# Hybrid HGRN2 and Mamba-2 layer: row sums of squares in quarters of a PSUM bank with their roots by way of DRAM, the first block's splits on VectorE, inputs loaded one step ahead

## Chip, core and metric

One core of a Trainium2 chip runs the whole layer in one launch. The metric is device time in microseconds (us) of one execution; a smaller time is better. TensorE (PE) multiplies, VectorE (DVE), ScalarE (ACT) and GpSimd (POOL) work elementwise, and SyncE (SP) only issues DMAs, one after the other.

## What is computed

One decoder layer over 2048 tokens of width 1024, all in float32. An RMS norm, one input projection, two mixers side by side (an HGRN2 gated linear recurrence with 8 heads, and a Mamba-2 scan with 16 heads in two groups), each with a norm and a gate of its own, one output projection, the residual, a last RMS norm. Cut to what matters:

```python
h = rmsnorm(x, norm_w[l])
proj = jnp.einsum('bsd,de->bse', h, w_in[l])
q_raw, f_raw, i_raw, g_raw, z, xbc, dt_raw = jnp.split(proj, split_idx, axis=-1)
hg_out = hgrn2_mix(...)    # o * rsqrt(mean(o*o over a head's 128) + EPS) ...
m2_out = mamba2_mix(...)   # y * rsqrt(mean(y*y over a group's 512) + EPS) ...
mix = jnp.concatenate([hg_out, m2_out], axis=-1)
x = x + jnp.einsum('bse,ed->bsd', mix, w_out[l])
return rmsnorm(x, final_norm_w)      # rmsnorm: x * rsqrt(mean(x*x over 1024) + EPS) * w
```

Three kinds of row sums of squares occur ahead of the output projection: over 1024 of the input (one for each token), over 128 of each HGRN2 head, and over 512 of each Mamba-2 group.

## The kernel before

**Tiles.** Tokens lie along the free axis, 512 to a block, four blocks. Each 128 columns of the input projection are one weight tile; `proj` (L376) multiplies it with the block's input as 24 matmuls of 128x512. Float32 is kept by splits: a value is cast to a high part (ACT) and the rest is a subtraction (DVE or POOL), and three products of parts are added: high with high, low weight with high input, high weight with low input. `hh` and `hl` are the parts of the input, `wh` and `wl` those of a weight. In the first block the weights come raw from DRAM (`wr`), are split in `w_emit` (L128 is the subtraction; GpSimd does it for the Mamba-2 tiles and for one more) and are saved to DRAM; later blocks load the parts.

**Units.** A block is a list of jobs (`block_jobs`): `H(hd)` is one HGRN2 head (projections `pf`, `pq`, `pg`), `M(ct)` two Mamba-2 heads (`px`, `pz`), `VV(q)` the values of four HGRN2 heads (`pv`, four steps over four banks), `B(g)` a Mamba-2 group's B and C (`pB`, `pC`), `dt_unit` its time steps (`dt`). Each unit gives projections at once and later stages with due numbers (`DUES`, `MDUES`), counted in projections: stage `m0` of a head runs 3 projections after the head began, and so on. A head's stages are two levels of products inside a chunk (bank `A` by `m0b`, bank `B` by `m2`), a transpose `kT` (`mk`), the state `hS` (`m5`) and the output `o` (`m6`). Tile's scheduler then sets each engine's final order.

**First block.** Its first head runs on input that is not yet normed (`hr`, `lr`), since the row factors aren't ready: `row_factors` sums the squares on ACT and DVE, `ss` is the sum over partitions on PE, two POOL steps make the root, and `spread_factors` makes the row vector `rawrs` by a matmul with a diagonal (`dg_hr`, bank `hb`). Then `prep(0, x0)` scales the input and splits it anew (`x`, `hh`, `hl`) before `dt` can start.

**Next block's input.** While a block runs, `stats(tb+1)` (L319) loads the next input (`xa`), squares it and adds it up, and `prep(tb+1)` (L339) loads it again (`xb`), scales it by the row factors `prs` and splits it. Both take their loads where they use them, from the pool of three `raw` buffers that the weights use too. `prs` comes from a diagonal and a matmul (bank `hb`).

**Row sums.** `ss_cols` (L144) makes four 128x2 matmuls with the squares as the stationary operand, for the input (`ss`) and for each Mamba-2 group (`mss`). The Mamba-2 roots lie in `nst`, are transposed (`rgt`) and go to DRAM (`rg_store`, L931). The HGRN2 heads do it another way (`m7`, L883): four heads' sums in four quarters of one bank (`hss`, 32 columns of 1/128 each as stationary operand), one row of each quarter to DRAM, back folded over 128 partitions, the root on POOL, and back to DRAM, from where the output projection reads it spread over partitions.

The four output blocks follow the mixers; their matmuls are `po`.

Of the kernel before, what the change touches and what calls it, by code (L numbers as in the profile page):

```python
# [38 lines left out]
def hybrid_layer(ctx, tc, xT, wt, wdt, wout, small, out):
# [36 lines left out]
    mean32 = cp.tile([P, 32], F32, name="mean32")  # L76
    G.memset(mean32, 1.0 / P)
# [37 lines left out]
    def w_emit(i):  # L115
# [12 lines left out]
        (G if i == 2 or c >= 32 else V).tensor_tensor(lo, raw, hi.bitcast(F32), op=ALU.subtract)  # L128
# [190 lines left out]
    def stats(tb):  # L319

        box = {}

        def part(c):
# [15 lines left out]
    def prep(tb, xs=None):  # L339
# [3 lines left out]
        def part(c):  # L343
            if c == 0:
                if xs is None:
# [4 lines left out]
                else:  # L350
# [9 lines left out]
            for k in range(2):  # L360
# [146 lines left out]
    def m2_unit(tb, g, c, ws, bcs, dts, sq, nst, r):  # L507
# [760 lines left out]
```

## Time and profile before

| | |
|---|---|
| time, median of 3 runs | 1876.06 us (1873.55 to 1876.25) |
| profiled execution, its own time | 1876.26 us |
| its span, first to last instruction | 1874.5 us |
| PE busy | 1840.6 us, 98% of the span |
| DVE busy | 1204.3 us, 64% |
| ACT busy | 735.7 us, 39% |
| POOL busy | 315.3 us, 17% |
| mean granted TensorE clock | 0.993 of full speed |

Busy times are of one engine each and overlap. An instruction on PE that had to wait shows how long PE stood idle before it and which instruction of which engine released it. The page's strip of the granted clock shows full speed in nearly every slice, 9 tenths or less in the first and 8 tenths in the second.

### The profile page before, as it was taken

What the parts mean: (1) busy time and instruction counts of PE and PEld (TensorE: products, weight loads), DVE (VectorE), ACT (ScalarE), POOL (GpSimd) and SP (SyncE); (2) the same over time, 40 slices, a digit from 0 to 9 for tenths busy, and PEclk for the clock granted to TensorE, in tenths of its full rate; (3) what the DMA queues carried; (4) which work ended last, traced back from release to release, by engine and by line L of the source; (5) the groups of instructions that cost most, each with busy time, mean ns of one, the idle gap of its engine ahead of it and who ended that gap; (6) DMA issues with size and microseconds to landing.
All of it is one profiled execution on the core that took longest, in us unless ns stands there. A gap on an engine that the chain in (4) does not pass through costs nothing.

```text
span 1874.5 us, 33134 instructions
## 1 busy us (share of the span) xinstructions
PE 1840.6 (98%) x12910; PEld 1519.9 (81%) x12910; DVE 1204.3 (64%) x2951; ACT 735.7 (39%) x1303; POOL 315.3 (17%) x388
## 2 busy tenths in 40 slices
PE   7899999899999999999999999999999999999997
PEld 5688888788888888888888888888888877888887
DVE  7678868956576478556764885476457764534445
ACT  4546545533353245234433543353333532211113
POOL 1432243311011212120112221201121130000000
PEclk9899999999999999999999999999999999999999
DMA  7676877754555556456555655555565375424241
GB/s 277 245 274 233 299 258 251 257 182 157 176 187 202 180 180 225 142 176 191 175 201 182 194 195 202 171 191 166 172 193 168 113 235 171 163 84 154 92 148 46
DMA packets 112605, 351.83 MB, mean 188 GB/s; under 512 B 14464, under 2 KB 17184, under 8 KB 111936
## 3 DMA queue, kind: packets, MB, share of 16 engines
q1 hardware_dynamic: 111344, 348.46, 55.3%
q8 instruction: 102, 1.67, 0.4%
q10 hardware_dynamic: 1104, 1.26, 0.2%
q14 instruction: 55, 0.45, 0.1%
HBM read 269.69 MB, written 79.97 MB: 187 GB/s over the span
## 4 chain that ended last, share of the span: by engine, by line
PE 91%; DVE 5%; DMA 2%; issue 1%; ACT 1%; POOL 0%; DVEq 0%; SPq 0%; ACTq 0%
PE po L1100 16%; PE pz L384 9%; PE px L384 9%; PE pg L384 9%; PE pf L384 9%; PE pq L384 8%; PE pv L629 8%; PE pB L384 2%; PE pC L384 2%; PE yd L578 2%; PE yo L589 1%; PE hS L856 1%; PE S L569 1%; PE o L875 1%; PE o L874 1%; PE A L691 1%
## 5 line engine op out<-in xcount | busy, mean ns | idle before, releaser
L1100 PE MATMUL po<-mh,woh 128*128 128x512 f32 x480 | 188.9, 395 | 0.1
L1100 PE MATMUL po<-mh,wol 128*128 128x512 f32 x480 | 186.8, 390 | 0.0
L1100 PE MATMUL po<-ml,woh 128*128 128x512 f32 x480 | 186.1, 390 | 0.8 <-DVE ml L1089 0.8
L1100 PEld LDWEIGHTS po<-mh,woh 128*128 128x128 f32 x480 | 90.1, 188 | 22.0 <-issue 1.7
L828 POOL COPY att<-atq 32x128 f32<-32x128 f32 x128 | 63.2, 493 | 261.1 <-DVE atq L713 257.2
L1100 PEld LDWEIGHTS po<-ml,woh 128*128 128x128 f32 x480 | 89.9, 188 | 20.5 <-DVE ml L1089 1.9
L1100 PEld LDWEIGHTS po<-mh,wol 128*128 128x128 f32 x480 | 90.1, 188 | 18.9 <-issue 0.7
L1088 ACT CAST mh<-mr 128x1024 fp32r<-128x1024 f32 x33 | 34.6, 1051 | 166.3 <-PE po L1100 146.5
L471 DVE SCALAR_TENSOR_TENSOR xs<-u_x,sm,xs 128x512 f32<-128x512 f32 x96 | 71.9, 749 | 14.5 <-ACT xs L469 14.2
L542 DVE TENSOR_SCALAR csb<-csb,cs 128x128 f32<-128x128 f32 x256 | 65.2, 327 | 23.9 <-ACT ecs L539 23.9
L1089 DVE TENSOR_TENSOR ml<-mr,mh 128x1024 fp32r<-128x1024 f32 x31 | 37.8, 1220 | 65.6 <-ACT mh L1088 65.6
L865 DVE SCALAR_TENSOR_TENSOR hSt<-hgS,totw,hS 128x128 f32<-128x128 f32 x32 | 11.1, 346 | 95.4 <-PE hS L856 95.4
L629 PE MATMUL pv<-wh,hh 128*128 128x512 f32 x224 | 71.2, 399 | 0.0
L629 PE MATMUL pv<-wl,hh 128*128 128x512 f32 x224 | 69.5, 391 | 0.0
L629 PE MATMUL pv<-wh,hl 128*128 128x512 f32 x224 | 69.0, 389 | 0.0
L384 PE MATMUL px<-hh,wh 128*128 128x512 f32 x256 | 68.4, 410 | 0.0
L384 PE MATMUL pz<-hh,wh 128*128 128x512 f32 x256 | 67.4, 405 | 0.0
L601 POOL TENSOR_TENSOR sqa<-sqa,ecs 128x512 f32<-128x512 f32 x24 | 34.2, 1424 | 190.4 <-ACT ecs L600 190.4
L384 PE MATMUL pg<-hh,wh 128*128 128x512 f32 x248 | 65.4, 405 | 0.0
L384 PE MATMUL pf<-hh,wh 128*128 128x512 f32 x248 | 64.7, 403 | 0.0
L384 PE MATMUL pq<-hh,wh 128*128 128x512 f32 x248 | 64.7, 401 | 0.0
L128 POOL TENSOR_TENSOR wl<-wr,wh 128x1024 fp32r<-128x1024 f32 x21 | 53.8, 2563 | 64.6 <-ACT wh L127 63.3
(356 smaller groups left out, 4635.1 us busy)
## 6 DMA issues: line engine op xcount, KB each, us to landing
wh<-whd SPq DMA_DIRECT2D x156, 512.0 KB, 4.4
wl<-wld SPq DMA_DIRECT2D x156, 512.0 KB, 3.5
whd<-wh SPq DMA_DIRECT2D x52, 512.0 KB, 4.7
wld<-wl SPq DMA_DIRECT2D x52, 512.0 KB, 3.9
wr<-wt SPq DMA_DIRECT2D x51, 512.0 KB, 5.1
mr<-mixd SPq DMA_DIRECT2D x66, 256.0 KB, 2.9
csb<-csd SPq DMA_DIRECT2D x32, 512.0 KB, 5.6
rgh<-rgd SPq DMA_DIRECT2D x34, 256.0 KB, 3.2
```

The source lines that it names most:

```text
L128: (G if i == 2 or c >= 32 else V).tensor_tensor(lo, raw, hi.bitcast(F32), op=ALU.subtract)
L384: state["mm"] = T.matmul(ps, lhsT=a[:, k, :], rhs=b[:, k, :], start=(n == 0), stop=(n == 23))
L471: V.scalar_tensor_tensor(dst, u[:, j:j + TB], cw[:, c, j:j + 1], dst, op0=ALU.mult, op1=ALU.add)
L542: V.tensor_scalar(csb[:, i, w, :], csb[:, i, w, :], dts["cs"][:, w, h0 + i:h0 + i + 1], 0.0, ALU.subtract, ALU.min)
L569: T.matmul(pS[:, sl], lhsT=bc["Bn"][:, w, :], rhs=xdc[:, sl], start=True, stop=True)
L578: T.matmul(pd[64 * i:64 * i + 64, w * P:(w + 1) * P], lhsT=xdt[:, w * P + i * 64:w * P + i * 64 + 64], rhs=csb[:, i, w, :], start=True, st ...
L601: G.tensor_tensor(sq["acc"], sq["acc"], t, op=ALU.add)
L629: T.matmul(ps, lhsT=a[:, 2 * j + k, w * P:(w + 1) * P], rhs=rhs, start=(j == 0 and n == 0), stop=(j == 3 and n == 5))
L828: G.tensor_copy(att[qs, :, qs], r["atq"][qs])
L1088: A.copy(mh[:, :, 0:n], mr[:, :, 0:n])
L1089: lo.tensor_tensor(ml[:, :, 0:n], mr[:, :, 0:n], mh[:, :, 0:n].bitcast(F32), op=ALU.subtract)
L1100: T.matmul(pss[d], lhsT=a[:, d, :], rhs=b, start=(first and n == 0), stop=(e == (HE - 1 if bl == LAST else 15) and n == 2))
```

## The change

All sums of squares but the first block's input go the way of the heads: one function, `row_roots`, takes up to four sums, puts each into a quarter of a bank by a matmul with 32 columns of 1/n, and takes the roots by way of DRAM. The next input's sum shares a bank with the first Mamba-2 group's; the second group's goes alone, in the last block with the first's. The row factors `prs` are read from DRAM, spread over partitions, and no longer made by a diagonal and a matmul. The input parts of `stats` and `prep` are loaded one step ahead of their use. In the first block all weight splits and the low parts of the normed input are on DVE, the first head's later stages have due numbers of their own, the row factors are made inside `pg`, `dt` has a bank of the larger pool, and the last step of `VV` ends its four banks in another order.

```diff
+RDUES = (3, 4, 7, 9, 10, 11, 12, 13)
...
-        (G if i == 2 or c >= 32 else V).tensor_tensor(lo, raw, hi.bitcast(F32), op=ALU.subtract)
+        V.tensor_tensor(lo, raw, hi.bitcast(F32), op=ALU.subtract)
...
+    def row_roots(nm, tb, row, accs, keep):
+        n = len(accs)
+        ps = bank(nm)
+        for j, (acc, m) in enumerate(accs):
+            T.matmul(ps[32 * j:32 * j + 32, :], lhsT=means[m], rhs=acc, start=True, stop=True)
+        A.copy(keep[0:32 * n, :], ps[0:32 * n, :])
+        flat = rg_d[tb][row * NW:(row + n) * NW, :].rearrange("w t -> (w t)")
+        nc.sync.dma_start(flat.rearrange("(j t) -> j t", j=n),
+                          keep[0:32 * n, :].rearrange("(j r) t -> j r t", r=32)[:, 0, :])
+        rc = mp.tile([P, 16], F32, tag="rc", bufs=2, name=f"rc{nm}")[:, 0:NW * n]
+        fold = flat.rearrange("(p c) -> p c", c=NW * n)
+        nc.sync.dma_start(rc, fold)
+        rstd_cols(rc, rc, 1)
+        nc.sync.dma_start(fold, rc)
...
     stats:
-                x_rstd(tb, ss_cols(acc, bank(f"ss{tb}")))
-        return [lambda c=c: part(c) for c in range(4)]
+                row_roots(f"ss{tb}", tb - 1, R0, [(sq[0]["acc"], 512), (acc, D)], acc)
+        def at(c):
+            load(c + 1)
+            if c >= 0:
+                part(c)
+        return [lambda c=c: at(c) for c in range(-1, 4)]
...
     prep:
-                    ps = bank(f"hb{tb}")
-                    bcast_cols(rsx[:, tb, :], None, ps, f"h{tb}")
-                    box["rs"] = slot("s", [TB], f"prs{tb}")
-                    A.copy(box["rs"], ps)
...
-                E = V if kk % 2 else G
+                E = V if kk % 2 or xs is not None else G
...
+        def at(c):
+            if xs is None and c < 0:
+                box["rs"] = slot("s", [TB], f"prs{tb}")
+                nc.sync.dma_start(box["rs"].rearrange("p (w t) -> p w t", w=NW),
+                                  rg_d[tb - 1][RX * NW:(RX + 1) * NW, :].partition_broadcast(P))
+            if xs is None and c < 3:
+                box[c + 1] = xr = wp.tile([P, 2, TB], F32, tag="raw", bufs=3, name=f"xb{tb}_{c + 1}")
+                nc.sync.dma_start(xr, xT[tb, :, 2 * c + 2:2 * c + 4, :])
+            if c >= 0:
+                part(c)
...
     proj:
+                if inside and n == 12:
+                    inside()
...
     dt_unit:
-            ps = pj.tile([P, TB], F32, tag="pj", name=f"dt{tb}")
+            ps = bank(f"dt{tb}")
...
     m2_unit:
         def m3():
-            ssv = ss_cols(sq["acc"], bank(f"mss{nm}"))
-            ss = mp.tile([P, NW], F32, tag="mss", bufs=2, name=f"mss{nm}")
-            V.tensor_copy(ss, ssv)
-            rstd_cols(nst[:, g, :], ss, 512)
+            accs = [(sq["acc"], 512)]
+            if tb == NTB - 1:
+                accs.append((sqs[0]["acc"], 512))
+            row_roots(f"mss{nm}", tb, R1, accs, sq["acc"])
...
     v_step:
-            for w in ((1, 2, 0, 3) if tb in raw_rs else range(NW)):
+            for w in ((0, 3, 1, 2) if j == 3 else (1, 2, 0, 3) if tb in raw_rs else range(NW)):
...
     hg_unit:
-            row_factors(tb, x0)
...
-            held["g"] = proj(hts[tb], w_get(ws[2]), f"pg{nm}", bank(f"pg{nm}"))
+            held["g"] = proj(hts[tb], w_get(ws[2]), f"pg{nm}", bank(f"pg{nm}"), lambda: row_factors(tb, x0))
...
-        return [pf_raw, pq_raw, pg_raw] if raw else [pf, pq, pg], list(zip(DUES, (m0, m0b, m1, m2, mk, m5, m6, m7)))
+        return [pf_raw, pq_raw, pg_raw] if raw else [pf, pq, pg], list(zip(RDUES if raw else DUES, (m0, m0b, m1, m2, mk, m5, m6, m7)))
...
-        add(rg_store, tb, nst)
```

**Where the first block's first head ends.** PE, from the last values' matmuls on: `B` is the head's second level, `kT` its transpose, `dt` the first use of the normed input, `pB` the next projection. Before:

```order
L629 MATMUL pv_0_3_557<-wh_629,lr_307 128x512 x2
L691 MATMUL B_0_772<-MB_0_0_661,k_0_528 32x48 x16
L819 MATMUL B_0_772<-hq_0_672 32x32 x8
L823 MATMUL B_0_772<-qa_0_673,k_0_485 64x64 x4
L403 MATMUL dt_818<-hh_533,wd 32x512 x8
L403 MATMUL dt_818<-hl_534,wd 32x512 x8
L390 MATMUL kT_0_837<-ident,k_0_485 128x128 x4
L384 MATMUL pB_0_892<-hh_533,wh_698 128x512 x4
```

And with the change:

```order
L666 MATMUL pv_0_2_556<-wh_629,lr_307 128x512 x2
L439 MATMUL dt_772<-hh_533,wd 32x512 x8
L439 MATMUL dt_772<-hl_534,wd 32x512 x8
L418 MATMUL pB_0_839<-hh_533,wh_667 128x512 x4
L451 MATMUL dtn_791<-sel,dT_789 128x16 x4
L418 MATMUL pB_0_839<-hh_533,wh_667 128x512 x4
L418 MATMUL pB_0_839<-hh_533,wl_668 128x512 x8
L418 MATMUL pB_0_839<-hl_534,wh_667 128x512 x8
L727 MATMUL B_0_874<-MB_0_0_741,k_0_528 32x48 x16
```

`dt` and `pB` now come before `B`, and `kT` (not shown) stands after `pC`.

The same place on DVE, where `x` is the scaling of the normed input, `hl` its low part, `wl` a weight's split, and `MB`, `tot`, `k` belong to the head's second level. Before:

```order
L365 TENSOR_TENSOR hl_534<-x_1_297,hh_533 128x512
L713 COPY_PREDICATED atq_0_617<-mask_506,A_0_584 128x16x4
L771 TENSOR_TENSOR MB_0_0_661<-MB_0_0_523,tot_0_0_526 128x16x4x2
L773 TENSOR_TENSOR MB_0_0_661<-MB_0_0_523,tot_0_0_526 128x16x4x4
L721 TENSOR_TENSOR tot_0_0_526<-tot_0_0_526 128x64
L362 SCALAR_TENSOR_TENSOR x_2_300<-x_2_300,sm,rawrs_482 128x512
L722 TENSOR_TENSOR tot_0_0_526<-tot_0_0_526 128x64
L362 SCALAR_TENSOR_TENSOR x_2_300<-x_2_300,sm,rawrs_482 128x512
```

And with the change:

```order
L388 TENSOR_TENSOR hl_534<-x_1_297,hh_533 128x512
L385 SCALAR_TENSOR_TENSOR x_2_300<-x_2_300,sm,rawrs_482 128x512 x2
L131 TENSOR_TENSOR wl_668<-wr_669,wh_667 128x1024
L388 TENSOR_TENSOR hl_534<-x_2_300,hh_533 128x512 x2
L385 SCALAR_TENSOR_TENSOR x_3_303<-x_3_303,sm,rawrs_482 128x512 x2
L131 TENSOR_TENSOR wl_706<-wr_707,wh_705 128x1024
L388 TENSOR_TENSOR hl_534<-x_3_303,hh_533 128x512 x2
L807 TENSOR_TENSOR MB_0_0_741<-MB_0_0_523,tot_0_0_526 128x16x4x2
```

The whole normed input is split before the second level begins; two weight splits and all low parts, which POOL had a share of, stand among it.

**Where the first block's last heads run.** SP's queue around the load of the last part of the next input, `xb_3`; `mixd` are stores of finished outputs, `whd` and `wld` saves of weight parts. Before:

```order
L94 DMA whd_131<-wh_3859 128x1024
L880 DMA mixd_0_226<-sg_0_3130 128x512
L95 DMA wld_183<-wl_3860 128x1024
L595 DMA mixd_0_258<-y_0_3663 128x512
L356 DMA xb_3_4004<-xT 128x1024
L328 DMA xa_0_6089<-xT 128x1024
```

And with the change:

```order
L399 DMA xb_3_3786<-xT 128x1024
L97 DMA whd_95<-wh_3692 128x1024
L129 DMA wr_3798<-wt 128x1024
L98 DMA wld_147<-wl_3693 128x1024
L129 DMA wr_3849<-wt 128x1024
L97 DMA whd_119<-wh_3796 128x1024
```

The load has moved ahead of three more weight loads and of the stores of `sg` and `y`.

DVE ahead of the last head's `k`, which `kT` on PE needs; `csb` is a Mamba-2 decay. Before:

```order
L743 TENSOR_TENSOR tot_7_0_3997<-f_0_3806 128x256
L362 SCALAR_TENSOR_TENSOR xb_3_4004<-xb_3_4004,sm,prs_3369 128x512 x2
L542 TENSOR_SCALAR csb_0_3587<-csb_0_3587,cs_997 128x128 x8
L365 TENSOR_TENSOR hl_3372<-xb_3_4004,hh_3371 128x512
L546 TENSOR_TENSOR csb_0_3587<-csb_0_3587,BC_0_2697 128x1024
L713 COPY_PREDICATED atq_0_3698<-mask_515,B_0_3894 128x4x24
L833 TENSOR_TENSOR k_0_3382<-k_0_3382,tot_6_0_3796 128x4x64
```

And with the change:

```order
L779 TENSOR_TENSOR tot_7_0_3985<-f_0_3794 128x256
L579 TENSOR_SCALAR csb_0_3575<-csb_0_3575,cs_974 128x128 x8
L131 TENSOR_TENSOR wl_3939<-wr_3940,wh_3938 128x1024
L583 TENSOR_TENSOR csb_0_3575<-csb_0_3575,BC_0_2685 128x1024
L749 COPY_PREDICATED atq_0_3686<-mask_515,B_0_3882 128x4x24
L869 TENSOR_TENSOR k_0_3370<-k_0_3370,tot_6_0_3784 128x4x64
```

The two `xb` steps and the `hl` stand further ahead in the queue now, and one weight split stands here instead.

## Rows read from the trace of the kernel before

**Rows 1.** The page's first part: busy time of each engine.

```profile
PE 1840.6 (98%) x12910; PEld 1519.9 (81%) x12910; DVE 1204.3 (64%) x2951; ACT 735.7 (39%) x1303; POOL 315.3 (17%) x388
```

**Rows 2.** PE's timeline, first 80 us: start, duration, instruction, count, [idle before].

```profile
21.55 1.98 PE L384 MATMUL pq<-lr,wh 128*128 128x512 f32 x8
25.17 1.02 PE L148 MATMUL ss<-ones,pacc 128*128 128x2 f32 x8 [1.65 <-DVE pacc L303]
26.05 3.67 PE L384 MATMUL pg<-hr,wh 128*128 128x512 f32 x8
...
33.20 1.02 PE L168 MATMUL hb<-dg_hr,ones 128*128 128x512 f32 x2
...
61.09 0.44 PE L819 MATMUL B<-hq 128*32 128x32 f32 x16 [2.75 <-DVE hq L797]
...
65.09 3.59 PE L403 MATMUL dt<-hh,wd 128*32 128x512 f32 x8 [2.38 <-ACT v L635]
...
71.59 1.17 PE L384 MATMUL pB<-hh,wh 128*128 128x512 f32 x4
```

**Rows 3.** DVE's timeline, first 70 us.

```profile
17.20 2.90 DVE L303 TENSOR_TENSOR pacc<-pacc,sq 128x512 f32<-128x512 f32 x1
...
27.82 0.88 DVE L167 TENSOR_SCALAR dg_hr<-ident,rsx 128x128 f32<-128x128 f32 x4 [1.06 <-POOL rsx L142]
...
48.82 2.79 DVE L365 TENSOR_TENSOR hl<-x,hh 128x512 fp32r<-128x512 f32 x1
...
51.66 0.28 DVE L771 TENSOR_TENSOR MB<-MB,tot 128x128 f32<-128x128 f32 x1
...
61.80 1.24 DVE L806 TENSOR_TENSOR tot<-tot 128x8 f32<-128x8 f32 x1
```

**Rows 4.** Line 128, weight splits: count, ns min/median/max, first and last start.

```profile
L128 DVE TENSOR_TENSOR wl<-wr,wh x30: 1204/1220/2237, 15.3 to 351.4; 128x1024 fp32r<-128x1024 f32 x30
L128 POOL TENSOR_TENSOR wl<-wr,wh x21: 2375/2401/3387, 16.3 to 363.8; 128x1024 fp32r<-128x1024 f32 x21
```

**Rows 5.** Windows: length, busy PE, PEld, DVE, ACT, POOL; clock, DMA.

```profile
34.88:65.08 30.20, 24.27 (x214) 19.15 (x213) 29.59 (x56) 14.00 (x26) 13.19 (x6) 0.92 0.58 209
190.00:220.00 30.00, 30.00 (x278) 25.38 (x277) 27.89 (x65) 14.70 (x23) 10.82 (x6) 1.00 0.79 283
```

**Rows 6.** PE's timeline near the first block's end.

```profile
372.58 1.12 PE L390 MATMUL kT<-ident,k 128*128 128x128 f32 x4 [4.74 <-DVE k L833]
373.70 3.75 PE L384 MATMUL px<-hh,wh 128*128 128x512 f32 x8
```

**Rows 7.** DVE's timeline at the same place.

```profile
363.46 3.55 DVE L362 SCALAR_TENSOR_TENSOR xb<-xb,sm,prs 128x512 f32<-128x512 f32 x2 [1.98 <-DMA xb<-xT]
```

**Rows 8.** SP's queue at the same place.

```profile
358.77 0.45 SPq L356 DMA_DIRECT2D xb<-xT  x1
```

**Rows 9.** PE's timeline around row sums and a spread in the first block.

```profile
243.74 1.07 PE L890 MATMUL hss<-on,mean 128*32 128x512 f32 x8
...
250.32 0.95 PE L148 MATMUL mss<-ones,sqa 128*128 128x2 f32 x8
251.13 0.63 PE L390 MATMUL tB<-ident,BT 128*128 128x128 f32 x4
...
317.93 1.02 PE L168 MATMUL hb<-dg_h,ones 128*128 128x512 f32 x2
318.39 2.16 PE L384 MATMUL pq<-hh,wh 128*128 128x512 f32 x7
```

**Rows 10.** DMA issues: queue, count, KB each, us to landing.

```profile
rc<-rgd SPq DMA_DIRECT2D x8, 8.0 KB, 3.1
rgh<-rgd SPq DMA_DIRECT2D x34, 256.0 KB, 3.2
```

**Rows 11.** POOL's timeline: the root of four heads' sums.

```profile
257.93 2.89 POOL L142 TENSOR_TENSOR rc<-rc,mhalf 128x16 f32<-128x16 f32 x1
```

**Rows 12.** PE's waits by what it waited for: total, times, longest.

```profile
PE yo L589 <- DVE hgS L865: 2.1, 1, 2.1
```

More of the change, by code (lines that the diff above doesn't have):

```diff
@@ L75, in hybrid_layer @@
     G.memset(mhalf, -0.5)
-    mean32 = cp.tile([P, 32], F32, name="mean32")
-    G.memset(mean32, 1.0 / P)
+    means = {}
+    for n in (P, 512, D):
+        means[n] = cp.tile([P, 32], F32, name=f"mean{n}")
+        G.memset(means[n], 1.0 / n)
     epst = cp.tile([P, 1], F32, name="epst")
@@ L317, in scaled, with stats, load @@
         return dst
-    def stats(tb):
+    def stats(tb, sq):
         box = {}
+        def load(c):
+            if c < 4:
+                box[c] = xr = wp.tile([P, 2, TB], F32, tag="raw", bufs=3, name=f"xa{tb}_{c}")
+                nc.sync.dma_start(xr, xT[tb, :, 2 * c:2 * c + 2, :])
         def part(c):
@@ L344, in part @@
             if c == 0:
[L345 to L350 removed]
+                if xs is not None:
                     box["rs"] = raw_rs[tb]
@@ L367, in part @@
                 new_hts[tb] = (hh, hl)
-        return [lambda c=c: part(c) for c in range(4)]
+        def at(c):
[8 more added lines that the diff above has]
+                part(c)
+        return [lambda c=c: at(c) for c in range(-1, 4)]
     new_hts = {}
@@ L374, in use, with proj @@
         hts[tb] = new_hts[tb]
-    def proj(h, w, name, ps=None):
+    def proj(h, w, name, ps=None, inside=None):
         hh, hl = h
@@ L887, in m7 @@
                 return
-            ps = bank(f"hss{nm}")
-            for j in range(4):
-                T.matmul(ps[32 * j:32 * j + 32, :], lhsT=mean32, rhs=sqs[j], start=True, stop=True)
-            rr = sqs[3]
-            A.copy(rr, ps)
-            flat = rg_d[tb][(hd - 3) * NW:(hd + 1) * NW, :].rearrange("w t -> (w t)")
-            nc.sync.dma_start(flat.rearrange("(j t) -> j t", j=4), rr.rearrange("(j r) t -> j r t", r=32)[:, 0, :])
-            rc = mp.tile([P, 16], F32, tag="rc", bufs=2, name=f"rc{nm}")
-            fold = flat.rearrange("(p c) -> p c", c=16)
-            nc.sync.dma_start(rc, fold)
-            rstd_cols(rc, rc, 1)
-            nc.sync.dma_start(fold, rc)
-        return [pf_raw, pq_raw, pg_raw] if raw else [pf, pq, pg], list(zip(DUES, (m0, m0b, m1, m2, mk, m5, m6, m7)))
+            row_roots(f"hss{nm}", tb, hd - 3, [(a, P) for a in sqs], sqs[3])
+        return [pf_raw, pq_raw, pg_raw] if raw else [pf, pq, pg], list(zip(RDUES if raw else DUES, (m0, m0b, m1, m2, mk, m5, m6, m7)))
     pend = []
@@ L990, in block_jobs @@
         M(4)
+        call(nxt[4])
+        nxt = prep(tb + 1) if tb + 1 < NTB else [lambda: None, lambda: None, early_mix, lambda: None, lambda: None]
         H(5)
-        nxt = prep(tb + 1) if tb + 1 < NTB else [lambda: None, early_mix, lambda: None, lambda: None]
+        call(nxt[0])
         M(5)
-        call(nxt[0])
+        call(nxt[1])
         H(6)
-        call(nxt[1])
+        call(nxt[2])
         M(6)
-        call(nxt[2])
+        call(nxt[3])
         H(7)
-        call(nxt[3])
+        call(nxt[4])
         M(7)
-        add(rg_store, tb, nst)
         return out_
@@ L1027, in hybrid_layer @@
     low_part(0, x0)
-    again = prep(0, x0)
+    again = prep(0, x0)[1:]
     def consts():
```

32 lines of the change are left out of this document (11 added, 21 removed).

## Prediction

> **What bounds the kernel now.** I read the page's busy times first: PE is busy 98% of the span, DVE 64%, POOL 17% [rows 1]. So a microsecond goes only where PE stands idle, runs at half its clock, or has less to do. PE's timeline says where it is idle: in the first 70 us, ahead of `ss` (1.65), ahead of the second level's `B` (2.75) and ahead of `dt` (2.38) [rows 2], and once near the first block's end, ahead of `kT` (4.74) [rows 6]. By the table of waits, what remains is short, the longest 2.1 ahead of the last block's `yo` [rows 12]. Third, the clock: eight 128x512 matmuls take 3.67 in `pg` right after the first wait, but 1.98 in `pq` before it [rows 2]; half the clock, as after `kT` (3.75) [rows 6]. Last come the engines that PE waits for: DVE is busy 29.59 of the 30.20 us in which the first block's input is normed, POOL works beside it [rows 5], and the weight splits are shared by the two [rows 4].
>
> The sum is made against the profiled execution, 1876.26 us, 1.76 more than its span; the median of the runs is 1876.06.
>
> **A. The first 72 us.** `pq` ends at 23.53 (21.55 + 1.98) [rows 2]. `ss` is now issued inside `pg`, so `pg` starts there, unbroken by the wait and so at the full clock, which I take as 3.67 / 2 = 1.84 for eight. `ss` stands behind 15 of its 24 matmuls, at 23.53 + 15 x 0.229 = 27.0. It finds its operand ready: `pacc` ended shortly before 25.17 [rows 2]; two splits newly ahead of it on DVE add 2.4 [rows 4]; but one `pacc` took 2.90 [rows 3] where a 128x1024 split, twice its size, takes 1.22 [rows 4], so some 2.2 of it was POOL's split in the way, and goes. 25.1 + 2.4 - 2.2 = 25.3, under 27.0; with the stretch kept, 27.5, half a microsecond of wait. The chain from `ss` by the POOL root to the diagonal's end takes what it took, 25.17 to 28.70 (27.82 + 0.88) [rows 2, 3], 3.5: `hb` at 30.5, not 33.20. PE's stretch from `hb` to the values' end lasted to 61.09 - 2.75 = 58.34, 25.1, of which some 0.5 is a group of `B` that now comes later (I take the 0.44 of the next one); hence 55.2 [rows 2]. `dt` no longer waits for its bank. Its 16 matmuls take 16 x 0.229 = 3.7 at the full clock, not 3.59 for eight [rows 2]: `pB` starts at 58.9, not 71.59, 12.7 earlier. Owed afterwards are 28 small products of `B` (at 0.44 for 16: 0.8) [rows 2] and `kT` (half its 1.12) [rows 6], 1.3. **A = 11.4.**
>
> That needs DVE in time. `f` began 1.7 after `hb`, at 34.88 [rows 2, 5], so now at 32.2. Of the 30.2 us that followed, the second level leaves: 20 instructions from `MB` at 51.66 to `tot` at 61.80 [rows 3], 8.9 by their durations, 4.3 of it stretched in the same way. POOL's stretch of one split (2237 against 1220) [rows 4] and one `hl` (2.79 against some 0.6 for half a split's elements) [rows 3] goes, 3.2. Four low parts and two splits come, 4 x 0.6 + 2 x 1.2 = 4.8. So 30.2 - 8.9 - 3.2 + 4.8 = 22.9, and the last `hl` is there at 55.1. `dt` wants it in its second half, at 57.0: 1.9 to spare. The second level follows after `dt` and `pB`, and its output has `pC` and the next unit as cover. Bounds: if no stretch goes but falls on other steps, the last `hl` comes 3.2 + 4.3 later, 62.6, and 5.6 of A is lost, leaving 5.8; if `B`'s products also cost nothing more, 12.7. I stay at 11.4, the value of the rows at hand.
>
> **B. The wait for `kT`.** `k` on DVE was late by 4.74 [rows 6]. In its queue ahead of it DVE waited 1.98 for a load of `xb` and then scaled it for 3.55 [rows 7]; SP had issued that load only at 358.77, behind stores of finished outputs [rows 8]. The change puts the load a step ahead, and the two `xb` steps and the `hl` leave this place; one split of 1.2 comes in [rows 4]: 1.98 + 3.55 - 1.2 = 4.3 of the 4.74 go, and 0.4 stays. With the wait the half clock behind it goes: 3.75 - 1.98 in `px`, half of `kT`'s 1.12 [rows 2, 6], 2.3. 4.3 + 2.3 = 6.6; I add 0.3, since part of 0.4 may fall to `hl`. **B = 6.9.** Bounds: 7.1 (all gone), and 3.5 when half of it turns up again as a wait for another DVE step, since DVE has the same work to do somewhere.
>
> **C. PE's own work on row sums.** Removed: 8 `mss` and 3 `ss`. One of them took 0.95, but kept the next instruction back by 0.81 (250.32 to 251.13); a spread `hb` by 0.46 (317.93 to 318.39), three go; the transposes `rgt` some 0.1 [rows 9]. 11 x 0.81 + 3 x 0.46 + 0.1 = 10.4. Added: four pairs and three singles. No row shows them; the nearest are four quarters at 1.07 (`hss`) and one full-width matmul of the same 512 columns at 0.46 [rows 9]. Eight passes in a row would be 8 x 0.23 = 1.84, so quarters overlap, at 1.07 for four. I take 0.46 for a single and 0.66 for a pair (a third of the way from one to four): 4.0. **C = 10.4 - 4.0 = 6.4.** Bounds: 7 x 0.46 = 3.2 and 7 x 1.07 = 7.5, so 7.2 to 2.9.
>
> The Trainium skill speaks against the low price ("TensorEngine Tiling (Array Packing)", Tiling Modes, Key Properties): tiles work independently and in parallel, and a switch of the tiling mode drains TensorE. By it one quarter costs what four do, and most of 1.07 is the drain. The overlap of four quarters agrees; what one costs no row shows. The gain would be 3.5 less.
>
> **What I cost at nothing.** Splits on DVE: 21 x 1.22 = 25.6 comes in over the first block [rows 4]. A window of it shows DVE busy 27.89 of 30 us, so 2.1 free, and POOL 10.82 [rows 5]; but the 21 POOL splits took 2.4 each, in which DVE's own steps were stretched (1.0 in the longest split, 2.2 in one `hl`) [rows 3, 4]. At 1.2 lost for each the exchange is even, and I take it so. Without that, rival 2. The roots by DRAM: a store, a load, a root, a store, a spread load, each landing in 3.1 to 3.2 [rows 10], with POOL's 2.89 [rows 11]: some 16 us. SP issues in order, so weight loads behind a waiting store wait too; in the first block they are issued well over ten us ahead of use, and the heads' chain already has such a store. The sums of the input are done some 20 us before `prep` reads `prs`. The last wait of the kernel, `yo` (2.1) [rows 12], isn't touched; for the range it may go.
>
> **Sum.** 11.4 + 6.9 + 6.4 = 24.7; 1876.26 - 24.7 = **1851.6**.
>
> **Rivals.**
> *One quarter costs like four (1855.1).* C is 2.9: 1876.26 - 11.4 - 6.9 - 2.9. For it: only the four together are on record. Against it: nothing but the full-width 0.46. By the Trainium skill's rule above this is the case that holds.
>
> *Waits move rather than leave (1860.5).* DVE's long steps are not POOL's doing, or ACT or a load is late next: A is 5.8, B 3.5, C 6.4. For it: DVE is full in this stretch [rows 5], and 1.9 is a thin margin. Against it: the long steps stand where POOL's splits run.
> The Trainium skill ("SBUF — State Buffer", SBUF: two separate sides) calls the port pair that DVE and GpSimd share a lock held for a whole instruction, the other blocked; the 2.90 of `pacc` agrees, and by that rule the stretch goes with POOL's splits and this rival falls.
>
> *DVE becomes the bound of the first block (1874.6, the same).* If the splits' 25.6 us on DVE are not paid back by shorter steps, its 2.1 in 30 cover 23 over some 330 us when evenly spread, and nothing where it is full already. Between 2.6 and 25.6 I take 14.1: 1860.5 + 14.1. The change then does not do what it says for the splits. Against it: the 2237 of one split.
>
> *The root's chain holds SP's queue (1880, slower).* Four DMAs for each of three `prs`, each held in SP's queue behind another transfer: 4 x (3.2 + 3.2 + 1) + 2.9 = 32.5 rather than 16 [rows 10, 11], 12.5 past the 20 at hand; with the wait's half clock some 9.5 of it is PE's, for three blocks 28.5. 1851.6 + 28.5 = 1880.1; slower from 9.5 per block. Against it: the loads ahead were issued early, and a late `prs` delays only `prep`, which has several units of cover.
>
> **How the numbers follow.** 0.2% of the time, 3.75 us, is about what a measurement of this kernel can tell from no change. Forecast 0.52, quarters 0.14, moved waits 0.20, DVE as the bound 0.06, SP's queue 0.06, better than all bounds 0.02. Low: 1876.26 - 12.7 - 7.1 - 7.2 - 2.1 = 1847.2, which I round to 1847. High: A 5.8, B 3.5 and C 2.9 together give 1864.1, which I put at 1864. Outside lie 0.14. Faster 0.88, same 0.06, slower 0.06.
>
> **What would show it.** A: no wait ahead of `ss`, `pg` at 1.98 for eight, `pB` near 59, the clock's strip full in its second slice; wrong if PE waits for `hl` or for `v` ahead of `dt`. B: `kT` waits under 0.5 and `px` is at 1.98; wrong if a wait of some us stands anywhere in 340 to 380. C: the PE rows of the pair and the single, and what follows them by 0.46, 0.66 or 1.07. Splits: none on POOL, no DVE split above some 1.3. SP: an `rc` load that waits long with PE idle behind it would be the slower rival. The forecast falls altogether if DVE's share of the first block rises and PE waits for `wl`.

## The result: 1855.6 us, 0.99 of the time before

| | before | after |
|---|---|---|
| median | 1874.87 us (1873.55 to 1876.25, 4 runs) | 1855.57 us (1854.14 to 1856.72, 4 runs) |
| ratio, 95% interval | | 0.9897 [0.9879, 0.9914] |
| span of the profiled run | 1874.5 us | 1854.0 us |
| PE busy | 1840.6 us | 1828.0 us |

The forecast was 1851.6 us, in a range of 1847 to 1864. The time lies in the range, 4.0 us above the forecast; 19 to 20 us went where 24.7 were forecast. The page after, first part and the strip of the granted clock:

```profile
PE 1828.0 (99%) x12834; PEld 1507.5 (81%) x12834; DVE 1191.5 (64%) x2953; ACT 732.5 (40%) x1297; POOL 263.7 (14%) x357
...
PEclk9999999999999999999999999999999999999999
```

POOL's busy time fell by 52 us, DVE's did not rise though it took over POOL's splits [rows 1], and the granted clock is at 9 tenths or more in every slice, the second too. Where the 20.5 us of span went is best read as a *lead*: the same projection is looked up in both PE timelines, and its start before minus its start after is what has been won by then.

| stretch, up to the start of | lead there | won in it |
|---|---|---|
| first `pf` (6.50 before, 7.65 after) | -1.15 | -1.15 |
| `pf` of the second head | 9.34 | 10.5 |
| `pq` of the first block's last head | 11.80 | 2.5 |
| `pz` behind the first block's `kT` | 19.03 | 7.2 |
| last `pz` of the fourth block | 23.50 | 4.5 |
| last sum of the output (`sumz`) | 20.82 | -2.7 |

The first line is no part of the change: in fourteen profiles of this study the first matmul starts between 6.0 and 7.7, by the wait for the first weight's high part, and the profile after is the latest of them. The second line is the prediction's term A, the fourth is B, the third and the fifth together are C in the main, and the last one is a loss that it didn't have.

PE's timeline after, first stretch (start, duration, instruction, count, [idle before]):

```profile
24.38 1.98 PE L418 MATMUL pg<-hr,wh 128*128 128x512 f32 x8
...
27.78 0.95 PE L151 MATMUL ss<-ones,pacc 128*128 128x2 f32 x8
...
31.32 1.12 PE L171 MATMUL hb<-dg_hr,ones 128*128 128x512 f32 x2 [0.44 <-DVE dg_hr L170]
...
55.49 1.99 PE L439 MATMUL dt<-hh,wd 128*32 128x512 f32 x8
...
59.13 1.07 PE L418 MATMUL pB<-hh,wh 128*128 128x512 f32 x4
...
74.92 0.44 PE L481 MATMUL cs<-xd,triu 128*128 128x64 f32 x2 [1.41 <-DVE xd L474]
```

Against [rows 2]: no wait ahead of `ss`, `pg` at 1.98 and not 3.67, no wait ahead of `dt`, `pB` at 59.13 and not 71.59. Two waits are new: 0.44 ahead of `hb` and 1.41 ahead of `cs`.

DVE after, the last two low parts of the first normed input:

```profile
53.54 1.35 DVE L388 TENSOR_TENSOR hl<-x,hh 128x512 fp32r<-128x512 f32 x2
```

The last ends at 54.89 (forecast 55.1), 0.68 each where [rows 3] has one of 2.79.

PE after, where [rows 6] has its wait, and DVE there:

```profile
355.90 0.60 PE L426 MATMUL kT<-ident,k 128*128 128x128 f32 x4
356.54 2.06 PE L418 MATMUL px<-hh,wh 128*128 128x512 f32 x8
```

```profile
349.36 1.66 DVE L579 TENSOR_SCALAR csb<-csb,cs 128x128 f32<-128x128 f32 x8
351.08 1.23 DVE L131 TENSOR_TENSOR wl<-wr,wh 128x1024 fp32r<-128x1024 f32 x1
```

`kT` doesn't wait, `px` runs at the full clock (granted clock 1.00); the 1.98 and 3.55 of [rows 7] are gone, one split of 1.23 is in.

PE after around a pair and a single of row sums:

```profile
265.09 0.62 PE L242 MATMUL ss<-sqa,mean 128*32 128x512 f32 x1
...
266.07 2.11 PE L418 MATMUL pf<-hh,wh 128*128 128x512 f32 x8
...
420.61 1.05 PE L242 MATMUL mss<-sqa,mean 128*32 128x512 f32 x2
421.59 0.43 PE L481 MATMUL cs<-xd,triu 128*128 128x64 f32 x2
```

The pair is the `ss` row and the rows left out behind it, the single is `mss`. In both the next instruction starts 0.98 later; behind the four quarters of `hss` in the kernel before it was 1.00 (433.06 to 434.06).

PE after at the last block's end, where the loss lies; then ACT and SP there:

```profile
1505.85 1.05 PE L242 MATMUL mss<-sqa,mean 128*32 128x512 f32 x4 [2.17 <-POOL sqa L638]
...
1521.18 0.49 PE L1116 MATMUL po<-mh,woh 128*128 128x512 f32 x1 [1.13 <-ACT woh L1065]
1522.44 0.80 PE L1116 MATMUL po<-mh,wol 128*128 128x512 f32 x1 [0.77 <-DVE wol L1066]
```

```profile
1520.08 2.94 ACT L1065 CAST woh<-wor 128x1024 fp32r<-128x1024 f32 x3 [12.50 <-DMA rgd<-rcmss]
```

```profile
1518.56 0.32 SPq L251 DMA_DIRECT2D rgd<-rcmss  x1
```

The 2.1 of `yo` [rows 12] is gone, but the last pair's sum comes late behind a low part of 3.33 on POOL, and the output weights' cast on ACT stands 12.50 us until the store of the last pair's roots has landed: the pool that the weights lie in takes over the memory of the roots.

### The profile page after: what moved, and what is told of

Same layout as the page of the kernel before. It is cut to its first block, busy times and chain, and to the rows that moved or that the text cites. A ratio compares the mean times of both kernels' runs of the same rounds, so it can differ in the third digit from the quotient of the medians.

```text
span 1854.0 us, 32964 instructions
## 1 busy us (share of the span) xinstructions
PE 1828.0 (99%) x12834; PEld 1507.5 (81%) x12834; DVE 1191.5 (64%) x2953; ACT 732.5 (40%) x1297; POOL 263.7 (14%) x357
## 4 chain that ended last, share of the span: by engine, by line
PE 90%; DVE 5%; DMA 3%; ACT 1%; issue 1%; POOL 1%; DVEq 0%; SPq 0%; ACTq 0%; POOLq 0%
PE po L1116 15%; PE pv L666 9%; PE pz L418 9%; PE pf L418 9%; PE px L418 9%; PE pq L418 9%; PE pg L418 8%; PE pB L418 2%; PE pC L418 2%; PE yd L615 2%; PE S L606 1%; PE hS L892 1%; PE o L911 1%; PE yo L626 1%; PE o L910 1%; PE A L727 1%
## 5 line engine op out<-in xcount | busy, mean ns | idle before, releaser
L864 POOL COPY att<-atq 32x128 f32<-32x128 f32 x128 | 75.4, 589 | 308.9 <-DVE atq L749 281.2
L579 DVE TENSOR_SCALAR csb<-csb,cs 128x128 f32<-128x128 f32 x256 | 61.3, 313 | 24.3 <-ACT ecs L576 24.3
L131 DVE TENSOR_TENSOR wl<-wr,wh 128x1024 fp32r<-128x1024 f32 x51 | 62.2, 1223 | 10.8 <-ACT wh L130 10.4
L418 PE MATMUL pz<-hh,wl 128*128 128x512 f32 x256 | 63.4, 390 | 0.0
```

Source lines behind the costliest of these rows:

```text
L131: V.tensor_tensor(lo, raw, hi.bitcast(F32), op=ALU.subtract)
L579: V.tensor_scalar(csb[:, i, w, :], csb[:, i, w, :], dts["cs"][:, w, h0 + i:h0 + i + 1], 0.0, ALU.subtract, ALU.min)
L864: G.tensor_copy(att[qs, :, qs], r["atq"][qs])
```

## The experiments

All times are medians beside runs of the kernel before on the same chip (1875.6 to 1876.4 there); the changed kernel is 1855.6. Theories are those of the expectations, written before each run.

### The splits: back on GpSimd, and alone on DVE

The changed kernel with

```diff
-        V.tensor_tensor(lo, raw, hi.bitcast(F32), op=ALU.subtract)
+        (G if i == 2 or c >= 32 else V).tensor_tensor(lo, raw, hi.bitcast(F32), op=ALU.subtract)
```

> The changed kernel with one thing undone: in the first block the 21 weight splits are on GpSimd again. Theory 1 (GpSimd's splits lengthen whatever DVE does meanwhile, so the exchange was even and only the tight first stretch paid): the last low part of the normed input comes 3 to 7 us later, PE waits 1 to 5 us ahead of dt or pB, and about nothing more later in the block: 1857 to 1861 us against 1855.6. Theory 2 (the splits on DVE cost their 25.6 us there, and some of it is PE's): faster than the changed kernel, 1846 to 1854 us. Theory 3 (neither matters, the order of the first head's second level did it): 1855.6 within 1.

Measured: 1864.02 us, ratio 0.9932 [0.9920, 0.9945]. Slower than the changed kernel by 8.4, more than theory 1 had, and not where it had it. By the leads against the changed kernel's trace 0.8 is lost in the first stretch and 9.2 between 293 and 375 us. PE there, and SP's queue:

```profile
362.56 0.66 PE L426 MATMUL kT<-ident,k 128*128 128x128 f32 x4 [1.84 <-DVE k L869]
363.69 3.57 PE L418 MATMUL px<-hh,wh 128*128 128x512 f32 x8 [0.47 <-DVE atq L749]
```

```profile
327.05 0.38 SPq L399 DMA_DIRECT2D xb<-xT  x1
```

So `kT` waits again although the last load is issued 31.7 us earlier than in [rows 8], and the half clock is back in `px` (granted clock 0.55 from 363.69 to 367.30). These two are not all of the 9.2: from 301 us on PE has four more waits, the longest 1.33 ahead of the `kT` of the head before, where the changed kernel has none.

The kernel before with the same line the other way:

```diff
-        (G if i == 2 or c >= 32 else V).tensor_tensor(lo, raw, hi.bitcast(F32), op=ALU.subtract)
+        V.tensor_tensor(lo, raw, hi.bitcast(F32), op=ALU.subtract)
```

> The kernel before with nothing but the 21 splits moved from GpSimd to DVE. Theory 1 (GpSimd's longer splits give the three raw buffers back late, so the last load of the next input starts late and DVE waits for it at the queue's head; with the splits on DVE the wait for kT goes without any load ahead): 1866 to 1869 us against 1875.6. Theory 2 (the load must be issued ahead, the splits only exchange one cost for another): 1874 to 1877. Theory 3 (they cost DVE 25.6 us and PE waits): above 1878.

Measured: 1867.10 us, 0.9954 [0.9942, 0.9965]: 8.5 us faster, as theory 1 said. By the leads 2.7 are won in the first stretch and 6.8 between 304 and 385 us. SP issues the last `xb` at 350.32, not 358.77 [rows 8]. The two runs agree: the move of the splits is worth some 8 us, most of it at the first block's end.

### The loads: at their use, and ahead without the splits

The changed kernel with

```diff
-            load(c + 1)
-            if c >= 0:
-                part(c)
-        return [lambda c=c: at(c) for c in range(-1, 4)]
+            load(c)
+            part(c)
+        return [lambda c=c: at(c) for c in range(4)] + [lambda: None]
...
-            if xs is None and c < 3:
-                box[c + 1] = xr = wp.tile([P, 2, TB], F32, tag="raw", bufs=3, name=f"xb{tb}_{c + 1}")
-                nc.sync.dma_start(xr, xT[tb, :, 2 * c + 2:2 * c + 4, :])
+            if xs is None and c >= 0:
+                box[c] = xr = wp.tile([P, 2, TB], F32, tag="raw", bufs=3, name=f"xb{tb}_{c}")
+                nc.sync.dma_start(xr, xT[tb, :, 2 * c:2 * c + 2, :])
```

> The changed kernel with the parts of the next input loaded where they are used, as before. Theory 1 (kT's wait of 4.74 us came from DVE waiting for the late load and then scaling the input ahead of k): the wait at the first block's end comes back with the half clock behind it, 1862 to 1863 us against 1855.6. Theory 2 (another part of the change, the lighter row sums or the splits, took the wait away): 1855.6 within 1.5.

Measured: 1857.94 us, 0.9900 [0.9885, 0.9916]; 2.4 us above the changed kernel, between the theories and nearer to the second. `kT` waits 1.43, not 4.74.

The kernel before with the new sums and the loads ahead, for which the changed kernel gets GpSimd's splits back and the first stretch of before:

> The kernel before with the new row sums and the loads one step ahead, splits and the first stretch as before; beside it stands the run with the sums alone, 1872.8. Theory 1 (as long as GpSimd's splits hold the raw buffers a load ahead of its use is worth little): 1871 to 1875. Theory 2 (the prediction's: the load ahead takes kT's wait away, 6.9 less): 1866.

Measured: 1872.14 us, 0.9980 [0.9971, 0.9989], beside 1872.81 for the sums alone (below): 0.7 us, within what the two sets of runs scatter. Theory 1. The waits for `kT` do get shorter (1.3 in all, against 3.8 in the run with the sums alone), but while GpSimd has the splits hardly any of it arrives in the time; a load ahead of its use is worth 0.7 to 2.4 us, not 6.9.

### A fourth buffer

Is it the raw buffers that GpSimd holds too long? The kernel before with

```diff
-tag="raw", bufs=3
+tag="raw", bufs=4
...
-            mr = o1.tile([P, 2, TB], F32, tag="mr", bufs=2, name=f"mr{bl}_{e}")
+            mr = o1.tile([P, 2, TB], F32, tag="mr", bufs=1, name=f"mr{bl}_{e}")
```

> The kernel before with four raw buffers instead of three, for which the outputs' row buffers go from two to one (that costs only behind 1465 us, where the outputs begin; what counts is the trace up to there). Theory 1 (GpSimd's splits hold the three raw buffers, so the last load of the next input starts late): the load is issued at 352 us or earlier, PE's wait for kT falls from 4.7 to under 1.5, and the last projection before the outputs starts 5 to 8 us earlier than the 1485.9 us of before. Theory 2 (the load starts late because it stands behind the stores of finished outputs in SP's queue, or DVE is simply full): the wait stays at 4 to 5, and 1485.9 within 2.

Measured: 1887.63 us, 1.0063 [1.0050, 1.0075], the loss behind 1465 us. Up to there the fourth buffer does half of what theory 1 said: SP issues the last `xb` at 346.31. But PE's waits only change their places:

```profile
364.32 2.11 PE L384 MATMUL pg<-hh,wh 128*128 128x512 f32 x8 [1.13 <-ACT k L669]
...
372.14 0.63 PE L390 MATMUL kT<-ident,k 128*128 128x128 f32 x4 [2.07 <-DVE atq L713]
```

and the last projection starts 0.8 us earlier than before, within theory 2's bound. DVE there, in the same run:

```profile
360.86 1.77 DVE L362 SCALAR_TENSOR_TENSOR xb<-xb,sm,prs 128x512 f32<-128x512 f32 x1
...
366.25 1.66 DVE L542 TENSOR_SCALAR csb<-csb,cs 128x128 f32<-128x128 f32 x8 [1.05 <-ACT ecs L539]
369.88 1.61 DVE L546 TENSOR_TENSOR csb<-csb,BC 128x1024 f32<-128x1024 f32 x1 [1.97 <-ACT csb L545]
```

The load was not all: DVE now has its input in time and is late by its own chain with ACT, in which a step of 0.74 still takes 1.77 beside a step of POOL. How much of the 7 us is the late buffer, how much the longer steps and how much ACT's order, these runs don't part. That the splits' place decides it they do show.

### The row sums: alone, and all quarters filled

The kernel before with the new row sums only (in the changed kernel, all else was put back):

> The kernel before with nothing but the row sums by quarters and their roots by way of DRAM: splits, loads and the first head's order are those of before. Theory 1 (the sums save PE 5 to 6 us in the four blocks, but at the last block's end the chain of the last pair's root, behind the heads' in SP's queue, holds back the output weights and costs 3 to 5): 1871.5 to 1875 us against 1874.9 before. Theory 2 (the prediction's term, 6.4 us and nothing lost): 1868.5 us. Theory 3 (the chain by DRAM costs PE waits in each block): above 1877 us.

Measured: 1872.81 us, 0.9981 [0.9972, 0.9990], 2.8 us faster: theory 1. By the leads 7.0 us are won up to the last `pz`, and the outputs from there to the last sum take 382.6 us, not 379.4. Of the 7.0, 1.3 are won between 325 and 385 us, where PE's waits for `kT` come to 3.8 in two, not 4.74 in one; that is not the sums' own price.

The changed kernel with

```diff
+        for j in range(n, 4):
+            T.matmul(ps[32 * j:32 * j + 32, :], lhsT=means[accs[0][1]], rhs=accs[0][0], start=True, stop=True)
```

> The changed kernel with every row sum's bank filled: where one or two quarters were used, the first sum is multiplied into the other two or three quarters too, 17 more matmuls of 32 columns, not read by anyone. Theory 1 (quarters run side by side, one costs PE what four cost, 0.98 us by the trace of the changed kernel): 1855.6 within 1. Theory 2 (the price that the prediction took, 0.46 for one rising to 1.07 for four, 0.2 for each quarter more): 17 x 0.2 = 3.4 more, 1859 us.

Measured: 1855.73 us, 0.9891 [0.9878, 0.9905], 0.2 from the changed kernel: theory 1. The pair with two idle quarters filled:

```profile
264.99 0.62 PE L242 MATMUL ss<-sqa,mean 128*32 128x512 f32 x1
265.00 0.62 PE L242 MATMUL ss<-pacc,mean 128*32 128x512 f32 x1
265.01 0.62 PE L244 MATMUL ss<-sqa,mean 128*32 128x512 f32 x2
...
265.99 2.12 PE L420 MATMUL pf<-hh,wh 128*128 128x512 f32 x8
```

All start within 0.02 and end together, and what follows starts 1.00 later, 0.98 with two quarters.

### The first stretch: as before, and the due numbers alone

The changed kernel with the first head's due numbers, the row factors' place, `dt`'s bank, the values' last step and GpSimd's share of the low parts as before:

> The changed kernel with the first stretch as before: the first head's second level ahead of the normed input's last splits, row factors ahead of pg, dt in the small pool, half of the low parts on GpSimd; splits on DVE, loads ahead and row sums are those of the change. Theory 1 (the new order alone makes the first stretch shorter, 10.5 us by the two traces from the first matmul on): 1864.5 to 1866.5 us against 1855.6. Theory 2 (the splits' move to DVE makes a good part of it, since it takes the long steps away): 1857 to 1861.

Measured: 1863.57 us, 0.9932 [0.9920, 0.9943]: 8.0 us slower, between the theories and 0.9 short of the first. `ss` waits 2.25 again and `pB` starts at 65.94, still 5.7 earlier than before; with nothing but the splits on DVE it was 65.52.

The changed kernel with the due numbers alone put back:

```diff
-        return [pf_raw, pq_raw, pg_raw] if raw else [pf, pq, pg], list(zip(RDUES if raw else DUES, (m0, m0b, m1, m2, mk, m5, m6, m7)))
+        return [pf_raw, pq_raw, pg_raw] if raw else [pf, pq, pg], list(zip(DUES, (m0, m0b, m1, m2, mk, m5, m6, m7)))
```

> The changed kernel with the first head's due numbers of before and nothing else undone. Theory 1 (the order on DVE, the normed input's splits ahead of the first head's second level, is what shortens the first stretch; row factors inside pg and dt's bank are worth the rest): 1859.5 to 1863 us against 1855.6, with waits of PE ahead of B. Theory 2 (the row factors inside pg and dt's bank do it): 1855 to 1857.5.

Measured: 1852.09 us, 0.9873 [0.9860, 0.9887], 3.5 us faster than the changed kernel, outside both theories: the new due numbers gain nothing and cost time. PE's three largest waits (what waited for what: total, times, longest):

```profile
PE pf L418 <- ACT wh L113: 7.7, 2, 6.6
PE mss L242 <- POOL sqa L638: 2.2, 1, 2.2
PE po L1116 <- DVE ml L1105: 1.7, 3, 0.7
```

The wait ahead of `cs` is gone: `xd`, which it needs, starts at 72.96 on DVE, not at 74.65, where the postponed second level stands ahead of it. By the leads, the start set aside, 1.6 us are won up to the second head. Another 1.3 are won in the outputs, where loads and engines have the same order as in the changed kernel; this part the runs don't explain. `dt` doesn't wait without the new numbers either.

### The tail

The changed kernel with the last roots in memory that stays, and the last sum of squares on DVE:

```diff
-        rc = mp.tile([P, 16], F32, tag="rc", bufs=2, name=f"rc{nm}")[:, 0:NW * n]
+        late = tb == NTB - 1 and row >= 4
+        rc = (cp.tile([P, 16], F32, name=f"rc{nm}") if late else
+              mp.tile([P, 16], F32, tag="rc", bufs=2, name=f"rc{nm}"))[:, 0:NW * n]
...
-                G.tensor_tensor(sq["acc"], sq["acc"], t, op=ALU.add)
+                (V if tb == NTB - 1 and ct == 7 else G).tensor_tensor(sq["acc"], sq["acc"], t, op=ALU.add)
```

> The changed kernel with two things altered at the last block's end: the folded roots of its last two row sums lie in memory that no later pool uses, so that the output weights' first high part has not to wait for their store; and the last sum of squares (sqa) is added on DVE, not on GpSimd behind a split of 3.3 us. Theory 1 (the trace's waits there, 2.17 for sqa, 1.13 and 0.77 for the output weights, and the half clock behind them, are the change's own late cost): 3.5 to 5 us less, 1850.5 to 1852. Theory 2 (something else, the outputs' own loads or low parts, is late next): 1854 to 1856.

Measured: 1856.33 us, 0.9895 [0.9882, 0.9908]: no gain, 0.3 above theory 2. The waits for `sqa` and `woh` are gone, and one longer wait has come; from the last `pz` to the last sum it takes 384.4 us, 382.1 in the changed kernel. PE and SP there:

```profile
1526.90 1.65 PE L1118 MATMUL po<-ml,woh 128*128 128x512 f32 x3 [7.52 <-DVE ml L1107]
```

```profile
1518.21 0.32 SPq L253 DMA_DIRECT2D rgd<-rcmss  x1
1518.64 0.37 SPq L1093 DMA_DIRECT2D rgh<-rgd  x1
```

A load of row factors (`rgh`) stands behind the last roots' store, which waits for POOL. With that chain on GpSimd's queue (`q.dma_start` for the three DMAs, `q = nc.gpsimd` in the last block):

> As the run on the tail before it (last roots in memory that no later pool uses, last sum of squares added on DVE), and the store, load and store of the last block's last two root chains are issued from GpSimd's own queue instead of SP's. Theory 1 (in that run a load of row factors for the outputs stood in SP's queue behind the last root's store, PE waited 7.5 us for what it feeds, and the half clock cost 2 more; on another queue nothing waits there): 1846 to 1849 us against 1856.3. Theory 2 (the loads of factors and weights would be late anyway): 1852 to 1857.

Measured: 1856.94 us, 0.9895 [0.9880, 0.9910]: again no gain, theory 2. SP issues the factors earlier, DVE gets them hardly earlier (1524.52, in the run before 1525.01):

```profile
1515.00 0.33 SPq L1182 DMA_DIRECT2D xo<-xT  x1
1515.74 0.32 SPq L1094 DMA_DIRECT2D rgh<-rgd  x1
```

```profile
1524.52 0.69 DVE L1095 TENSOR_TENSOR mr<-mr,rgh 128x512 f32<-128x512 f32 x1 [4.83 <-DMA rgh<-rgd]
```

8.8 us from issue to use, against 3.2 for such a load in [rows 10]: ahead of it runs the 2 MB load of the residual, `xo`. The unchanged time hides something, though. This profile is 2.8 us behind the changed kernel's at the last `pz` (the start set aside), nearly all of it lost between 308 and 360 us, where the edit doesn't reach and the engines work in the same order; from the last `pz` to the last sum it takes 381.7 us, 2.7 less than in the run before.

The last kernel holds the load of `xo` back, has the last roots and the last sum of squares as in the first of these two runs, puts only the roots' last store on GpSimd's queue, and takes the old due numbers. What is new in it:

```diff
-            if e == 6 and bl not in xos:
+            if e == (6 if bl else 10) and bl not in xos:
                 xos[bl] = op.tile([P, KT, TB], F32, tag="xo", bufs=1, name=f"xo{bl}")[:, :, 0:n]
+                if bl == 0:
+                    V.tensor_copy(xos[bl][:, 0, 0:1], mixes[bl, 10][0][:, 0:1].bitcast(F32))
```

> Best of what the runs pointed to: the changed kernel with the first head's due numbers of before (1852.1 alone), and at the last block's end the last roots in memory that no later pool uses, the last sum of squares added on DVE, the two root stores on GpSimd's queue, and the 2 MB load of the residual (xo) held back until the first output block's eleventh row, so that it no longer runs ahead of the loads of row factors. Theory 1 (the tail's waits come from what stands in or runs ahead of those loads: the stores in SP's queue and the 2 MB): the waits of PE between 1490 and 1545 us fall from some 5 to under 2, 1847 to 1849.5 us. Theory 2 (DVE's and ACT's own work on the outputs is late next, as in the two runs on the tail before): 1851 to 1853.

Measured: 1850.35 us, 0.9861 [0.9844, 0.9877], between the theories, and the fastest of all. A load of factors is now used 4.0 us after its issue. SP and DVE:

```profile
1510.35 0.32 SPq L1093 DMA_DIRECT2D rgh<-rgd  x1
```

```profile
1514.37 0.69 DVE L1094 TENSOR_TENSOR mr<-mr,rgh 128x512 f32<-128x512 f32 x1 [0.59 <-DMA rgh<-rgd]
```

Between 1490 and 1545 us one wait is left on PE, 3.85 for a cast of the mixed rows, not the under 2 of theory 1:

```profile
1519.29 0.50 PE L1118 MATMUL po<-mh,woh 128*128 128x512 f32 x1 [3.85 <-ACT mh L1106]
```

From the last `pz` to the last sum it takes 379.6 us, against 382.1 in the changed kernel and 379.4 before: the tail's loss is made good, not more. With the old due numbers alone it was 380.7, so the edits to the tail have some 1.1 of it.

## Why the prediction held, point by point

**A, 11.4 forecast, 10.5 measured.** The working stood nearly line by line: `ss` at 27.0 (27.78 with a start 1.15 later), the last `hl` at 55.1 (54.89), `pB` at 58.9 (59.13). What it left out is the wait of 1.41 ahead of `cs`: it gave the postponed second level "`pC` and the next unit as cover" and didn't look who else is behind it on DVE. At `pB` 13.6 us are won since the first `pf`, more than the 12.7 forecast; 3.1 of them are given back up to the second head, where the sum had 1.3. It also took the order as one piece. By the runs, the first stretch as before costs 8.0, the splits are 2.7 of the stretch when moved alone, and the new due numbers are a loss of some 1.6 there.

**B, 6.9 forecast, 7.2 measured, and the step behind it was wrong; that the numbers are so close is luck.** The prediction read "SP had issued that load only at 358.77, behind stores" and gave the wait to the load's place in the queue. Undoing the loads costs 2.4; adding them without the splits brings 0.7; the splits alone bring 6.8 us at this place and 8.5 in all. The splits, which the prediction costed "at nothing", are the term that carries it. A row at the place itself shows a part of how. In the kernel before, the two `xb` steps of 3.55 [rows 7] ran beside a split of POOL:

```profile
363.77 2.69 POOL L128 TENSOR_TENSOR wl<-wr,wh 128x1024 fp32r<-128x1024 f32 x1 [3.30 <-ACT wh L127]
```

Two `xb` steps at 0.74 each make 1.5, so some 2.1 us of the 3.55 are stretch in the chain to `k`. The prediction counted them as work that the earlier load takes out of the way, not as the splits'. What it had right of the splits is the exchange: from 70 to 250 us, where PE hardly waits, DVE's load hardly moves (137.13 of 180 us busy before, 136.56 with nothing but the splits moved, 138.06 after) and POOL's falls. At the block's end, where DVE's steps are on PE's path, it did not come out even. The window in the kernel before, with the splits alone, and in the kernel after (length, busy PE, PEld, DVE, ACT, POOL; clock, DMA):

```profile
70.00:250.00 180.00, 180.00 (x1277) 149.32 (x1276) 137.13 (x316) 98.77 (x157) 51.58 (x47) 1.00 0.74 262
70.00:250.00 180.00, 180.00 (x1277) 150.15 (x1276) 136.56 (x328) 99.72 (x158) 25.56 (x39) 0.99 0.74 263
70.00:250.00 180.00, 178.59 (x1276) 148.94 (x1275) 138.06 (x322) 102.02 (x165) 30.83 (x43) 1.00 0.75 260
```

The lock that the Trainium skill describes ("SBUF — State Buffer", SBUF: two separate sides) fits the long steps: from 72 to 290 us of the kernel before, the 21 instructions of DVE that ran beside one of POOL's 12 splits took 18.0 us more than the shortest of their form.

**C, 6.4 forecast, 7.0 measured for the sums alone up to the outputs, with errors against each other.** Without the 1.3 from `kT`'s waits 5.7 are left. Behind a pair and a single the next instruction starts 0.98 later, not 0.66 and 0.46; that is the rival "one quarter costs like four", 2.9 us worse. And a spread `hb` kept PE busy 0.9, not 0.46, which is nearer to the quarter's price: from a head's `pq` to its `pg` it is 7.80 us with the spread and 6.93 without. PE's timeline of the kernel before:

```profile
317.70 0.40 PE L384 MATMUL pq<-hh,wh 128*128 128x512 f32 x1
317.93 1.02 PE L168 MATMUL hb<-dg_h,ones 128*128 128x512 f32 x2
...
325.50 1.88 PE L384 MATMUL pg<-hh,wh 128*128 128x512 f32 x7
```

And of the kernel after:

```profile
307.53 1.98 PE L418 MATMUL pq<-hh,wh 128*128 128x512 f32 x8
...
314.46 1.86 PE L418 MATMUL pg<-hh,wh 128*128 128x512 f32 x7
```

The prediction took the distance between two recorded starts for the price [rows 9]; the matmul behind started inside the spread's own 1.02 by the record. A distance over a whole stretch with and without the instruction is safer. By it a pair costs more than its 0.98, too. From a head's `pz` to the next head's `pq`, before without a sum and after with the pair:

```profile
270.78 2.11 PE L384 MATMUL pz<-hh,wh 128*128 128x512 f32 x8
...
281.79 1.98 PE L384 MATMUL pq<-hh,wh 128*128 128x512 f32 x8
```

```profile
259.43 2.11 PE L418 MATMUL pz<-hh,wh 128*128 128x512 f32 x8
...
271.65 1.98 PE L418 MATMUL pq<-hh,wh 128*128 128x512 f32 x8
```

That is 11.01 and 12.22, so 1.21 for a pair. The old `ss` comes to 0.95 in the same way, not 0.81 (12.86 from the `pg` to the `pz` around it, 11.91 without). So the prices of what went and of what came were all too low, and 6.4 came out near the truth by chance. Of the Trainium skill's rule ("TensorEngine Tiling (Array Packing)", Key Properties) the parallel tiles are what the run with 17 more quarters shows, 0.2 us. A pair costs some 0.3 more than the full-width matmul of as many columns (1.21 against 0.87); whether that is the drain for the change of mode no run here shows.

**The tail, 0 forecast, 2.7 lost.** That `yo`'s wait "isn't touched" was the step that failed: it went (2.1), and some 4.8 came in its place (2.1 and the 2.7). The prediction weighed the roots' chain as a load on SP's queue in the blocks, where it costs nothing, and not at the last block's end, where the next stage's memory waits for its store. In the sums-alone run 3.3 of 7.0 us are given back there. Which part of the chain costs them is shown only in part: taking the two waits away brought another, and the loss went only with the load of `xo` held back and the old due numbers, in one run together.

**The rivals.** The one on quarters was right that one costs like four, and its 1855.1 is nearly the right time, but the time is right by chance: A, the rest of C and the tail are off in both directions. "Waits move rather than leave" holds in small: `cs` and the tail have new ones, `dt` and `kT` have none. SP's queue held by the roots cost PE no wait in the first three blocks. DVE did not become the bound.

## What to carry to other kernels

Before a wait is given to one instruction's place in a queue, look who holds the buffer that it fills and who else on that engine is slowed: here the helper engine's work was the cause, and the earlier load alone brought 0.7 us. Work given to a second elementwise engine is a gain only if its time isn't taken from the first; given back to DVE, it cost nothing in a slack stretch and won 7 us in a tight one. Look at the last iteration by itself: a chain that is hidden in every block may end on what the next stage allocates.

## What the runs showed of the hardware

Behind one, two or four quarters of 32 columns with 512 columns of float32 PE's next instruction started 0.98 to 1.00 us later alike, and 17 more quarters left the time as it was (0.2 us); over a stretch with and without it a pair came to 1.21, a full-width matmul to 0.87. Beside 12 splits of GpSimd, 21 steps of VectorE took 18.0 us more than the shortest of their form. A load of 256 KB that took 3.2 us as a median was used 8.8 us after its issue where a 2 MB load had been issued 0.7 us earlier, and 4.0 us after it with that load held back. The first matmul's start differs by up to 1.6 us between profiles of kernels that start alike.
